# A two-block transformer on one core: another order of work inside both mixers

## Chip, cores and metric

One core of a Trainium2 chip runs the whole kernel. The metric is the device time of one execution in microseconds (us); the time before is a median of three runs. The engines are TensorE (PE, its weight loads PEld), VectorE (DVE), ScalarE (ACT), GpSimd (POOL) and SyncE (SP, which issues most transfers).

## The reference

Batch 1, 256 tokens, width 1024, two layers of a first block and two of a second, all in fp32. What matters here are the two mixers:

```python
# first block, layer l: x = x + 0.5*ffn; x = x + mixer; x = x + 0.5*ffn; x = rmsnorm(x)
# mixer: one projection gives q, k, v (3 groups of 8 heads), the input of a gated convolution, and gates
for g, (window, dil) in enumerate(DILATION_GROUPS):
    o, l = dilated_window_attn(q[:, :, g], k[:, :, g], v[:, :, g], dil, window // (2 * dil))
y_conv = conv_module(glu_in, conv_w, conv_b, conv_ln_g, conv_ln_b, ...)   # 31 taps, layer norm, silu
return (g_attn * y_attn + g_conv * y_conv) @ w_out
# second block, layer l
p = rmsnorm_2(x, norm1[l]) @ w_in[l]          # columns: u (512), q (512), k (128), v (128)
y_f = fft2(u).real @ w_f + b_f                # Fourier half
y_a = windowed_gqa(rope(rmsnorm_2(q)), rope(rmsnorm_2(k)), v, sink[l])
x = x + concat([rmsnorm_2(y_f), rmsnorm_2(y_a)]) @ w_o[l]   # then a gated ffn
```

## The kernel before

Weights stream from HBM in units of 128x1024 fp32 (512 KB, issued on SP by `fetch`). Each unit is split in two fp32r halves: ACT writes the high half (`wh`, L317) and DVE the low half (`wl`, L318); PE then makes three products (low x high, high x high, high x low) of each operand. `token_major` (L576) is the form with tokens on the partitions: 512 output columns, four units of 12 matmuls, with two PSUM banks, one for each half t of the tokens.

**Order of the program.** The functions are written out in the order in which they should run; a scheduler places each instruction in its engine's queue, and each engine works through its queue in that order. So a step whose input is late blocks what is queued behind it on the same engine. PSUM has a ring of `acc` and one of `aux` banks; a matmul into a bank waits until the bank's last reader is done.

**Block one, `mixer` (L630).** After the gated convolution's input, nine projections run in the order of `QKV` (L47): each pair is (0 q, 1 k, 2 v; group). For q and k, `head_norm_rope` normalises each head and rotates it: squares on ACT, the factor `rs` by a power on POOL (L548), four DVE operations of 128x512 (L554, L556, L558, L560). Each half is then transposed on PE (`transpose_to`, L572), queued in `turn` until the next projection is through. v needs only one DVE operation for each half (L767). The convolution is a product with tables of cosines: `conv_forward` after projection 2, `conv_inverse(0)` after 4, `conv_inverse(1)` within 5 (L715 and L719 are its matmuls, L725 its last DVE operation). Its layer norm starts in the attention: `norm_mean` adds up eight blocks, takes the mean by one PE product with ones (L375), subtracts it (L734) and squares (L367, L368). The attention has steps of scores (L796), softmax on DVE and ACT (L803 to L811), transposes (L913, copied out by ACT in L915) and products with v (L821), with gate units between.

**Block two, `mixer2` (L923).** The stream gives q (four units), then k and v together (two units), then the Fourier half u (four units). `rc` and `vc`, the inverse norm and the mean square of each token, are taken before. q and k go through `head_norm_rope`, u is split into `uh` and `ul` (L346, L347). Then come, between the attention's steps (table `fill`): `f1`, the transform over the channels, `f2`, the one over the tokens (tables 2 x 512 KB in the stream, split like weights; its input `Ah`, `Al` split too, three fp32r products each, L1010 to L1030), the product with `w_f`, and the output projection. Before layer 0, `rf` and eight multiplications (L1279) make the residual. `sink`, eight numbers of the layer, comes by a POOL transfer into `nsink` (L929) and is copied on DVE (L931).

Of the kernel before, what the change touches and what calls it, by code (L numbers as in the profile page):

```python
# [23 lines left out]
F32 = mybir.dt.float32  # L24
# [4 lines left out]
P = 128  # L29
# [58 lines left out]
def weight_stream(a):  # L88
# [113 lines left out]
class Kernel:  # L202
# [64 lines left out]
    def make_units(self):  # L267
# [12 lines left out]
        for l in range(DEPTH):  # L280
# [3 lines left out]
            add("w", 16 + 4 * 3, 1024)  # L284
            add("d", 1, FWD)
            add("w", 4 * 6 + 16 + 4 + 8 + 8, 1024)
            add("w", 44, 1024)
            add_down()
        for l in range(DEPTH):
# [3 lines left out]
            add("d", 2, 1024)  # L293
# [282 lines left out]
    def token_major(self, o, evac, mid=()):  # L576
# [4 lines left out]
        for q in range(4):  # L581
# [9 lines left out]
            if q == 1:  # L591
                for f in mid:
                    f()
# [36 lines left out]
    def mixer(self, l, x, o, sacc, prep):  # L630
# [96 lines left out]
        def norm_mean():  # L727
# [26 lines left out]
        after = {2: conv_forward, 4: lambda: conv_inverse(0)}  # L754
        mid = {5: [lambda: conv_inverse(1)]}

        turn = []
        qT, kT, vv = [None] * 3, [None] * 3, [None] * 3
        for j, (which, g) in enumerate(QKV):
# [86 lines left out]
        for i in range(len(steps) + 2):  # L846
# [4 lines left out]
            gate(*gates.pop(0))  # L851
            if soft1 is not None:
# [70 lines left out]
    def mixer2(self, l, x, o, rc, vc, prep):  # L923
# [17 lines left out]
        nc.vector.tensor_scalar_mul(evc, vc, EPS)  # L941

        turn = []
# [7 lines left out]
        self.token_major(o, evac_q)  # L951
# [13 lines left out]
        todo, turn = turn, []  # L965
        for t in range(2):
            z = self.t2("z")
            nc.scalar.activation(z[:, :128], acc[t][:, :128], AF.Copy)
            nc.scalar.activation(vt[:, t * P:(t + 1) * P], acc[t][:, 128:256], AF.Copy, scale=rc[:, t:t + 1])
# [7 lines left out]
        Ah, Al = self.t4("Ah", F32R), self.t4("Al", F32R)  # L977
# [5 lines left out]
        def f1(hf):  # L983
# [14 lines left out]
            self.split(a.rearrange("p (b c) -> p b c", b=2), Ah[:, fb], Al[:, fb])  # L998


        def f2(i):


            wh, wl = self.unit(1024)
            a = self.acc()
            p, q, e = a[:, :130], a[:, 130:258], a[:4, 258:388]
            for fb in range(4):
                for cs, (out, ts) in enumerate(((p, slice(0, 130)), (q, slice(128, 256)))):
                    c = slice((fb * 2 + cs) * P, (fb * 2 + cs + 1) * P)
                    self.mm3(out, wh[:, c], wl[:, c], Ah[:, fb, ts], Al[:, fb, ts], fb == 0 and cs == 0, fb == 3, skip=True)  # L1010
# [3 lines left out]
            nc.scalar.activation(q_, q[:, 1:], AF.Copy)  # L1014
# [6 lines left out]
            if i == 0:  # L1021

                alt = dftu[0][0][:, 512:516]
                for fb in range(4):
                    for A in (Ah, Al):
                        mm(e, alt, A[:, fb, :130], start=False, stop=fb == 3 and A is Al, skip_group_check=True)
# [291 lines left out]
```

## Time and profile before

| | |
|---|---|
| median of 3 runs | 1970.82 us (1970.71 to 1971.87) |
| the profiled execution | 1971.52 us, span of the trace 1969.7 us |
| instructions | 36890 |
| busy: DVE, ACT, POOL | 1417.5 us (72%), 1100.1 us (56%), 110.9 us (6%) |
| read from HBM | 334.99 MB, 171 GB/s over the span |
| mean granted clock of TensorE | 0.992 of full |

How to read it: PE is the engine that is nearly always at work, so the time is its work plus its gaps, plus what it loses where its clock is granted at half. A gap is read from the wait rows, which name the engine, its line, and the instruction that released it.

### The profile page before, as it was taken

To read this page: it belongs to the slowest core of one execution; us is meant where nothing else is said; L and a number is where in the kernel's file an instruction comes from. 1 tells how busy PE (TensorE), PEld (TensorE's weight loads), DVE (VectorE), ACT (ScalarE), POOL (GpSimd) and SP (SyncE) were. 2 spreads that over 40 slices of the span, in tenths; PEclk is the share of its full clock that TensorE was granted. 3 is DMA by queue.
4 is the path that set the end of the run, shared out by engine and by line. 5 is a ranking of instruction groups with operands and counts; after the bars stand their busy time and mean duration, and the time that the engine had idled before them with its cause. 6 is when DMAs were issued, how large, how long until landed. Compare 5 with 4: busy or idle time off the path is not lost.

```text
span 1969.7 us, 36890 instructions
## 1 busy us (share of the span) xinstructions
PE 1929.9 (98%) x14640; PEld 1832.0 (93%) x14640; DVE 1417.5 (72%) x2470; ACT 1100.1 (56%) x2125; POOL 110.9 (6%) x109
## 2 busy tenths in 40 slices
PE   8999999999999999999999999999899999999999
PEld 8999878899999999998787999999789999889999
DVE  6765787877666586656877676665779985779973
ACT  5544555666544455445556665444676764666652
POOL 1000022100000010000222000000200000100000
PEclk9999999999999999999999999999989999999999
DMA  8555654435555555556544345555424555434554
GB/s 266 192 179 184 212 190 150 156 129 173 181 182 177 187 177 185 175 185 218 172 166 138 119 172 184 182 175 190 147 85 166 190 183 180 156 108 168 196 176 125
DMA packets 97260, 338.43 MB, mean 172 GB/s; under 512 B 11430, under 2 KB 14086, under 8 KB 96960
## 3 DMA queue, kind: packets, MB, share of 16 engines
q1 hardware_dynamic: 93024, 325.97, 48.7%
q0 software_dynamic: 2944, 8.11, 1.8%
q8 instruction: 114, 1.87, 0.4%
q10 hardware_dynamic: 1120, 2.00, 0.3%
q14 instruction: 58, 0.48, 0.1%
HBM read 334.99 MB, written 1.05 MB: 171 GB/s over the span
## 4 chain that ended last, share of the span: by engine, by line
PE 78%; DVE 8%; issue 6%; POOL 3%; ACT 3%; DMA 1%; POOLq 0%; DVEq 0%; ACTq 0%
PE acc L335 23%; PE acc L337 23%; PE acc L336 23%; POOL rs L548 3%; DVE wl L318 2%; PE acc L588 2%; PE acc L590 2%; PE acc L589 2%; ACT wh L317 1%; PE pt L913 1%; PE Y L821 1%; PE s L796 1%; DVE ra L554 1%; DVE rb L556 1%; ACT sq L367 1%
## 5 line engine op out<-in xcount | busy, mean ns | idle before, releaser
L318 DVE TENSOR_TENSOR wl<-raw,wh 128x1024 fp32r<-128x1024 f32 (+2 forms) x632 | 756.6, 1199 | 326.1 <-ACT wh L317 321.8
L317 ACT ACTIVATE wh<-raw 128x1024 fp32r<-128x1024 f32 (+2 forms) x632 | 653.2, 1037 | 595.2 <-PE acc L337 268.4
L335 PE MATMUL acc<-xh,wl 128*128 128x256 f32 x1760 | 503.8, 286 | 5.6 <-DVE wl L318 5.6
L336 PE MATMUL acc<-xh,wh 128*128 128x256 f32 x1760 | 499.8, 284 | 0.0
L337 PE MATMUL acc<-xl,wh 128*128 128x256 f32 x1760 | 499.3, 284 | 0.0
L335 PEld LDWEIGHTS acc<-xh,wl 128*128 128x128 f32 x1760 | 339.3, 193 | 9.3 <-DVE wl L318 6.0
L336 PEld LDWEIGHTS acc<-xh,wh 128*128 128x128 f32 x1760 | 339.4, 193 | 0.3
L337 PEld LDWEIGHTS acc<-xl,wh 128*128 128x128 f32 x1760 | 339.2, 193 | 0.0
L335 PE MATMUL acc<-hh,wl 128*128 128x256 f32 x1056 | 298.8, 283 | 0.0
L336 PE MATMUL acc<-hh,wh 128*128 128x256 f32 x1056 | 298.8, 283 | 0.0
L337 PE MATMUL acc<-hl,wh 128*128 128x256 f32 x1056 | 298.8, 283 | 0.0
L335 PEld LDWEIGHTS acc<-hh,wl 128*128 128x128 f32 x1056 | 202.8, 192 | 0.0
L336 PEld LDWEIGHTS acc<-hh,wh 128*128 128x128 f32 x1056 | 202.8, 192 | 0.0
L337 PEld LDWEIGHTS acc<-hl,wh 128*128 128x128 f32 x1056 | 202.8, 192 | 0.0
L588 PE MATMUL acc<-wl,xh 128*128 128x512 f32 x480 | 189.1, 394 | 0.8 <-DVE wl L318 0.5
L590 PE MATMUL acc<-wh,xl 128*128 128x512 f32 x480 | 187.3, 390 | 0.0
L589 PE MATMUL acc<-wh,xh 128*128 128x512 f32 x480 | 187.0, 390 | 0.0
L337 PE MATMUL acc<-xn,wh 128*128 128x256 f32 x608 | 172.7, 284 | 1.2 <-DVE xn L344 1.2
L335 PE MATMUL acc<-xn,wl 128*128 128x256 f32 x608 | 172.5, 284 | 0.0
L336 PE MATMUL acc<-xn,wh 128*128 128x256 f32 x608 | 172.0, 283 | 0.0
L337 PEld LDWEIGHTS acc<-xn,wh 128*128 128x128 f32 x608 | 116.6, 192 | 2.1 <-DVE xn L344 2.0
L335 PEld LDWEIGHTS acc<-xn,wl 128*128 128x128 f32 x608 | 116.7, 192 | 0.6 <-ACT xn L343 0.5
(276 smaller groups left out, 2926.6 us busy)
## 6 DMA issues: line engine op xcount, KB each, us to landing
raw<-wts SPq DMA_DIRECT2D x576, 512.0 KB, 3.3
raw<-wts SPq DMA_DIRECT2D x48, 384.0 KB, 3.0
brow<-b_in POOLq DMA_DIRECT2D x26, 256.0 KB, 3.9
raw<-dft SPq DMA_DIRECT2D x4, 512.0 KB, 3.5
tab<-tab ACTq DMA_DIRECT2D x1, 1024.0 KB, 7.5
out<-xn SPq DMA_DIRECT2D x8, 128.0 KB, 3.5
wraw<-conv_w POOLq DMA_DIRECT2D x6, 124.0 KB, 4.7
raw<-dft SPq DMA_DIRECT2D x2, 258.0 KB, 2.6
```

The costliest lines, as they stand in the source:

```text
L317: nc.scalar.activation(h[:, :n], r[:, :n], AF.Copy)
L318: nc.vector.tensor_tensor(lo[:, :n], r[:, :n], h[:, :n].bitcast(F32), op=ALU.subtract)
L335: mm(out, wl, xh, start=start, stop=False, **k)
L336: mm(out, wh, xh, start=False, stop=False, **k)
L337: mm(out, wh, xl, start=False, stop=stop, **k)
L367: nc.scalar.activation(q, x, AF.Square, **kw)
L548: nc.gpsimd.tensor_tensor(rs[:, :nh], vv[:, :nh], self.mhalf[:, :nh], op=ALU.pow)
L554: nc.vector.tensor_tensor(A3, z3, cg[:, None, :].to_broadcast([P, nh, HD]), op=ALU.mult)
L556: nc.vector.tensor_tensor(half(B[:, :nh * HD]), half(zz)[:, :, ::-1, :], sg.rearrange("p (c d) -> p c d", c=2)[:, None].to_broadcast([P, n ...
L588: mm(accs[t], xh[k][:, ts], wl[:, c], start=k == 0, stop=False)
L589: mm(accs[t], xh[k][:, ts], wh[:, c], start=False, stop=False)
L590: mm(accs[t], xl[k][:, ts], wh[:, c], start=False, stop=k == KB - 1)
```

## The change

Block one: the order of `QKV` puts each v between q and k; a projection's second transpose is held until two units of the next projection are through; the convolution's steps start one projection earlier (`conv_forward` after 1, the inverses after 3 and 4), its sum of blocks (`conv_sum`) and mean (`conv_mean`) follow at 4 and 6, so that only the subtraction is left in the attention. The last held transposes run after the first gate.

Block two: the weight stream and the program have the order q, Fourier half, k and v. The norm's sums (`stats`) are taken behind q's fourth unit, the residual behind the second unit of the Fourier half. `f1` and the transposes of q and k run before the attention's first step. The tables of `f2` are read as fp32 by two transfers of their own and are not split; `f1`'s result is one fp32 tile `A`; `f2` multiplies in fp32, once for each piece.

```diff
-QKV = [(0, 0), (1, 0), (2, 0), (2, 1), (0, 1), (1, 1), (0, 2), (1, 2), (2, 2)]
+QKV = [(0, 0), (2, 0), (1, 0), (0, 1), (2, 1), (1, 1), (0, 2), (1, 2), (2, 2)]
...
-        parts += [_wide(w[:, 512:1024]), w[:, 1024:].reshape(2, 4, P, 256).transpose(0, 2, 1, 3), _wide(w[:, :512])]
+        parts += [_wide(w[:, 512:1024]), _wide(w[:, :512]), w[:, 1024:].reshape(2, 4, P, 256).transpose(0, 2, 1, 3)]
...
-            add("d", 2, 1024)
...
-            if q == 1:
-                for f in mid:
-                    f()
+            for f in mid.get(q, ()):
+                f()
...
-        def norm_mean():
+        def conv_sum():
             cs = self.rp.tile([P, S], F32, tag="sacc", name=self.nm("cs"))
...
-            M = self.mean_rows(cs, D, 0.0)
+            stat["cs"] = cs
+
+        def conv_mean():
+            stat["cm"] = self.mean_rows(stat["cs"], D, 0.0)
+
+        def norm_mean():
             for b in range(KB):
-                nc.vector.tensor_tensor(cb(b), cb(b), M, op=ALU.subtract)
+                nc.vector.tensor_tensor(cb(b), cb(b), stat["cm"], op=ALU.subtract)
...
-        after = {2: conv_forward, 4: lambda: conv_inverse(0)}
-        mid = {5: [lambda: conv_inverse(1)]}
+        after = {1: conv_forward, 3: lambda: conv_inverse(0), 4: lambda: (conv_inverse(1), conv_sum()), 6: conv_mean}
...
-            self.token_major(o, evac, mid.get(j, ()))
-            for f in todo:
+            self.token_major(o, evac, {1: held})
+            held = todo[1:]
+            for f in todo[:1]:
                 f()
...
+            if i == 0:
+                for f in held:
+                    f()
...
-    def mixer2(self, l, x, o, rc, vc, prep):
+    def mixer2(self, l, o, stats, residual, prep):
...
+                t = self.t4("fw").rearrange("p a b -> p (a b)")
+                o_ = P * (FWD + INV + 516) + i * P * UMAX
+                nc.sync.dma_start(t, self.a["dft"][o_:o_ + P * UMAX].rearrange("(p n) -> p n", p=P))
...
-        self.token_major(o, evac_q)
+        self.token_major(o, evac_q, {2: [tables], 3: [start]})
+        self.token_major(o, lambda t, a: self.split(a, uh[t], ul[t], st["rc"][:, t:t + 1]), {1: [lambda: x.extend(residual())]})
...
-        self.token_major(o, lambda t, a: self.split(a, uh[t], ul[t], rc[:, t:t + 1]), todo)
-        for f in turn:
-            f()
...
-            self.split(a.rearrange("p (b c) -> p b c", b=2), Ah[:, fb], Al[:, fb])
+            nc.scalar.activation(A[:, fb], a.rearrange("p (b c) -> p b c", b=2), AF.Copy)
...
-                    self.mm3(out, wh[:, c], wl[:, c], Ah[:, fb, ts], Al[:, fb, ts], fb == 0 and cs == 0, fb == 3, skip=True)
+                    mm(out, w[:, c], A[:, fb, ts], start=fb == 0 and cs == 0, stop=fb == 3, skip_group_check=True)
...
-        fill = {0: [lambda: f1(0)], 1: [lambda: f1(1), lambda: f2(0)], 2: [lambda: f2(1), lambda: (f3(0), f3(1))],
-                3: [lambda: (f3(2), f3(3)), later("s", lambda: self.square_sum([yf[:, b] for b in range(4)]))],
+        fill = {0: [lambda: f2(0)], 1: [lambda: f2(1)], 2: [lambda: (f3(0), f3(1)), lambda: (f3(2), f3(3))],
+                3: [lambda: proj(0, 0), lambda: proj(0, 1), later("s", lambda: self.square_sum([yf[:, b] for b in range(4)]))],
...
+        f1(0)
+        for f in turn[:2]:
+            f()
+        f1(1)
+        for f in turn[2:]:
+            f()
...
+            return self.rsqrt_small(vc, 2), vc
+
+        def residual():
+            rf = self.rows(self.rsqrt_small(keep["v1"], 2))
```

Three places of the queues show it. In a row stand the line, the operation, what is written and what is read, and the shape. First DVE in block one's second layer, from the last rotation of k (L560) to the first softmax (L803, L809 after the change); `sink` is the copy of block two's eight numbers, L738 the subtraction of the mean, L368 the sum of squares. Before:

```order
L318 TENSOR_TENSOR wl_11917<-raw_11860,wh_11916 128x1024
L560 TENSOR_TENSOR z_11823<-ra_11839,rs_11837 128x512
L931 TENSOR_SCALAR sink_16013<-nsink_16011 128x8
L932 TENSOR_SCALAR nsink_16011<-nsink_16011 128x8
L318 TENSOR_TENSOR wl_11980<-raw_11878,wh_11979 128x1024
L318 TENSOR_TENSOR wl_12010<-raw_11896,wh_12009 128x1024
L767 SCALAR_TENSOR_TENSOR qkv_11857<-acc_11858,rc_10529,brow_11724 128x512
L767 SCALAR_TENSOR_TENSOR qkv_11857<-acc_11859,rc_10529,brow_11724 128x512
L318 TENSOR_TENSOR wl_12063<-raw_11914,wh_12062 128x1024
L803 ISA e_11964,m_11966<-s_11956,tab 128x512
```

Now, from the first softmax on:

```order
L318 TENSOR_TENSOR wl_12075<-raw_11926,wh_12074 128x1024
L809 ISA e_11970,m_11972<-s_11962,tab 128x512
L809 ISA m_11972 128x1
L809 ISA e_11971,m_11972<-s_11963,tab 128x512
L809 ISA m_11972 128x1
L738 TENSOR_TENSOR conv_11322<-conv_11322,var_11728 128x256
L811 TENSOR_SCALAR m_11972<-m_11972 128x2
L738 TENSOR_TENSOR conv_11322<-conv_11322,var_11728 128x256 x2
L368 TENSOR_TENSOR sacc_12124<-sacc_12124,sq_12126 128x256
L940 TENSOR_SCALAR sink_15980<-nsink_15978 128x8
L368 TENSOR_TENSOR sacc_12124<-sacc_12124,sq_12129 128x256
```

The copy of `sink` moved from ahead of four splits and the first softmax to behind it; subtractions and sums of squares moved in between the first softmax and the second.

Second, PE in block two's first layer where k is transposed (`tr` from `zk`, one for each half), with `f1` (L994 to L996 before, L1011 to L1013 now) and the scores (`s`). Before:

```order
L590 MATMUL acc_16242<-wh_16263,xl_15929 128x512
L572 MATMUL tr_16331<-ident,zk_16206 128x128 x2
L572 MATMUL tr_16335<-ident,zk_16225 128x128 x2
L994 MATMUL acc_16388<-wh_16293,uh_16016 128x256
L994 MATMUL acc_16434<-wh_16293,uh_16016 128x256
L995 MATMUL acc_16388<-wh_16293,ul_16017 128x256
```

Now:

```order
L1011 MATMUL acc_16366<-wh_16227,uh_15983 128x256
L1012 MATMUL acc_16366<-wh_16227,ul_15984 128x256
L1013 MATMUL acc_16366<-wl_16228,uh_15983 128x256
L572 MATMUL tr_16380<-ident,zk_16288 128x128 x2
L1026 MATMUL acc_16419<-A_16323,fw_16045 128x129
L572 MATMUL tr_16384<-ident,zk_16307 128x128 x2
L1026 MATMUL acc_16419<-A_16323,fw_16045 128x127
L1026 MATMUL acc_16419<-A_16323,fw_16045 128x129
L1026 MATMUL acc_16419<-A_16323,fw_16045 128x127
L1107 MATMUL s_16388<-kT_15986,qT_15985 128x256
```

`f1` stood behind the transposes of k and right behind u; it stands ahead of them now, with q's eight transposes, and the four units of u lie ahead of k and v.

Third, DVE at the same place: `zk` is k after its rotation, `sink` the copy for the layer after, `e` the first softmax. Before:

```order
L565 TENSOR_TENSOR zk_16225<-ra_16234,rs_16232 128x2x64 x2
L318 TENSOR_TENSOR wl_16385<-raw_16261,wh_16384 128x1024
L931 TENSOR_SCALAR sink_19616<-nsink_19614 128x8
L932 TENSOR_SCALAR nsink_19614<-nsink_19614 128x8
L318 TENSOR_TENSOR wl_16466<-raw_16291,wh_16465 128x1024
L347 SCALAR_TENSOR_TENSOR ul_16017<-acc_16241,rc_16009,uh_16016 128x512
L347 SCALAR_TENSOR_TENSOR ul_16017<-acc_16242,rc_16009,uh_16016 128x512
```

Now:

```order
L565 TENSOR_TENSOR zk_16288<-ra_16297,rs_16295 128x2x64 x2
L318 TENSOR_TENSOR wl_16596<-raw_16255,wh_16595 128x1024
L546 TENSOR_SCALAR vv_16312<-ss_16308,evc_15988 128x2
L554 TENSOR_TENSOR ra_16316<-z_16304,ropec_14000 128x128
L556 TENSOR_TENSOR rb_16317<-z_16304,ropes_14001 128x128
L558 TENSOR_TENSOR ra_16316<-ra_16316,rb_16317 128x128
L565 TENSOR_TENSOR zk_16307<-ra_16316,rs_16314 128x2x64 x2
L940 TENSOR_SCALAR sink_19562<-nsink_19560 128x8
L941 TENSOR_SCALAR nsink_19560<-nsink_19560 128x8
L1113 ISA e_16394,mx_16396<-s_16388,tab 128x256
```

The copy of `sink` stood ahead of `ul` and stands ahead of the first softmax now.

## Rows read from the trace of the kernel before

**Rows 1.** the page: busy us and share of engines; granted clock, 40 slices

```profile
PE 1929.9 (98%) x14640; PEld 1832.0 (93%) x14640; DVE 1417.5 (72%) x2470; ACT 1100.1 (56%) x2125; POOL 110.9 (6%) x109
...
PEclk9999999999999999999999999999989999999999
```

**Rows 2.** windows: stretch, length, busy of each engine, clock, DMA share, GB/s

```profile
345.00:393.00 48.00, 45.42 (x288) 39.37 (x287) 40.66 (x76) 32.57 (x105) 9.18 (x5) 1.00 0.48 160
1031.00:1079.00 48.00, 43.69 (x251) 36.63 (x250) 38.13 (x69) 30.36 (x101) 10.06 (x6) 0.93 0.48 159
1387.00:1425.00 38.00, 32.11 (x172) 26.44 (x171) 30.37 (x69) 26.22 (x79) 10.78 (x7) 0.99 0.41 134
1425.00:1450.00 25.00, 23.50 (x135) 19.34 (x136) 18.36 (x71) 16.06 (x49) 0.00 (x0) 0.74 0.24 85
1706.00:1738.00 32.00, 26.76 (x178) 21.43 (x177) 24.06 (x81) 20.78 (x58) 0.87 (x1) 0.95 0.39 132
```

**Rows 3.** timeline of PE, block one, layer 0: two waits, in brackets

```profile
371.58 0.63 PE L572 MATMUL tr<-ident,z 128*128 128x128 f32 x4 [1.12 <-DVE z L560]
...
386.75 0.71 PE L796 MATMUL s<-qkv,qkv 64*128 64x256 f32 x6 [1.46 <-ACT pT L915]
```

**Rows 4.** PE's waits in 1031 to 1079 (block one, layer 1)

```profile
PE sum L375 <- DVE m L803: 2.5, 1, 2.5
PE tr L572 <- DVE z L560: 1.1, 1, 1.1
PE s L796 <- ACT pT L915: 0.7, 1, 0.7
```

**Rows 5.** groups of instructions: count, busy us, mean ns, idle before

```profile
L368 DVE TENSOR_TENSOR sacc<-sacc,sq 128x256 f32<-128x256 f32 x110 | 45.0, 420 | 2.5
...
L715 PE MATMUL acc<-inv,Y 128*128 128x128 f32 x64 | 8.3, 277 | 2.9 <-DVE conv L725 2.9
```

**Rows 6.** timeline of PE, inverse convolution: start, length

```profile
315.54 1.95 PE L715 MATMUL acc<-inv,Y 128*128 128x128 f32 x16
```

**Rows 7.** timeline of PE, end of f1 and start of f2, layer 1

```profile
1716.64 0.28 PE L995 MATMUL acc<-wh,ul 128*128 128x256 f32 x1
1716.76 0.28 PE L996 MATMUL acc<-wl,uh 128*128 128x256 f32 x1
...
1717.16 0.27 PE L335 MATMUL acc<-Ah,wl 128*128 128x128 f32 x1
...
1717.72 0.27 PE L337 MATMUL acc<-Al,wh 128*128 128x130 f32 x1
```

**Rows 8.** timeline of POOL, block two, layer 0

```profile
1418.12 0.59 POOL L929 DMA_DIRECT2D nsink<-sink  x1
```

**Rows 9.** timeline of DVE, the same place

```profile
1418.61 1.22 DVE L318 TENSOR_TENSOR wl<-raw,wh 128x1024 fp32r<-128x1024 f32 x1
1422.66 0.17 DVE L931 TENSOR_SCALAR sink<-nsink 128x8 f32<-128x8 f32 x1 [2.83 <-DMA nsink<-sink]
...
1424.09 1.40 DVE L347 SCALAR_TENSOR_TENSOR ul<-acc,rc,uh 128x512 fp32r<-128x512 f32 x2
```

**Rows 10.** PE's waits in 1420 to 1450 (block two, layer 0)

```profile
PE acc L995 <- DVE ul L347: 2.7, 1, 2.7
PE acc L994 <- ACT uh L346: 2.1, 1, 2.1
```

**Rows 11.** PE's waits in 1706 to 1738 (block two, layer 1)

```profile
PE acc L335 <- ACT yfh L343: 1.7, 1, 1.7
PE pt L913 <- DVE e L1114: 1.1, 1, 1.1
```

**Rows 12.** timeline of ACT: k's second half leaves PSUM, layer 1

```profile
1702.26 0.26 ACT L968 ACTIVATE z<-acc 128x128 f32<-128x128 f32 x1
```

**Rows 13.** timeline of DVE: k's second half is done, layer 1

```profile
1708.17 0.49 DVE L565 TENSOR_TENSOR zk<-ra,rs 128x128 f32<-128x128 f32 x2 [0.27 <-POOL rs L548]
```

**Rows 14.** line 1279, the residual: count, shortest, median, longest in ns

```profile
L1279 DVE SCALAR_TENSOR_TENSOR xn<-xn,vec,R x8: 474/476/477, 1397.9 to 1400.6; 128x256 f32<-128x256 f32 x8
```

More of the change, by code (lines that the diff above doesn't have):

```diff
@@ L283, in make_units @@
             pos["d"] = 0
-            add("w", 16 + 4 * 3, 1024)
+            add("w", 16 + 4 * 2, 1024)
             add("d", 1, FWD)
-            add("w", 4 * 6 + 16 + 4 + 8 + 8, 1024)
+            add("w", 4 * 7 + 16 + 4 + 8 + 8, 1024)
             add("w", 44, 1024)
@@ L940, in mixer2, with start, tables @@
         evc = self.small("evc", 2)
-        nc.vector.tensor_scalar_mul(evc, vc, EPS)
-        turn = []
+        st, turn, x, fw = {}, [], [], []
+        def start():
+            st["rc"], vc = stats()
+            nc.vector.tensor_scalar_mul(evc, vc, EPS)
+        def tables():
+            for i in range(2):
+                t = self.t4("fw").rearrange("p a b -> p (a b)")
+                o_ = P * (FWD + INV + 516) + i * P * UMAX
+                nc.sync.dma_start(t, self.a["dft"][o_:o_ + P * UMAX].rearrange("(p n) -> p n", p=P))
+                fw.append(t)
         def evac_q(t, a):
@@ L964, in mixer2 @@
                     mm(acc[t][:, :256], xl[k][:, ts], wh[:, c], start=False, stop=k == KB - 1)
-        todo, turn = turn, []
         for t in range(2):
@@ L997, in f1 @@
             fb = slice(hf * 2, hf * 2 + 2)
-            self.split(a.rearrange("p (b c) -> p b c", b=2), Ah[:, fb], Al[:, fb])
+            nc.scalar.activation(A[:, fb], a.rearrange("p (b c) -> p b c", b=2), AF.Copy)
         def f2(i):
-            wh, wl = self.unit(1024)
+            w = fw[i]
             a = self.acc()
-            p, q, e = a[:, :130], a[:, 130:258], a[:4, 258:388]
+            p, q, e = a[:, :129], a[:, 129:256], a[:4, 256:385]
             for fb in range(4):
-                for cs, (out, ts) in enumerate(((p, slice(0, 130)), (q, slice(128, 256)))):
+                for cs, (out, ts) in enumerate(((p, slice(0, 129)), (q, slice(129, 256)))):
                     c = slice((fb * 2 + cs) * P, (fb * 2 + cs + 1) * P)
-                    self.mm3(out, wh[:, c], wl[:, c], Ah[:, fb, ts], Al[:, fb, ts], fb == 0 and cs == 0, fb == 3, skip=True)
+                    mm(out, w[:, c], A[:, fb, ts], start=fb == 0 and cs == 0, stop=fb == 3, skip_group_check=True)
+            if i == 0:
+                alt = dftu[0][0][:, 512:516].bitcast(F32)
+                for fb in range(4):
+                    mm(e, alt, A[:, fb, :129], start=False, stop=fb == 3, skip_group_check=True)
             y = self.t2("yF")
@@ L1013, in f2 @@
             q_ = y[:, 257:384]
-            nc.scalar.activation(q_, q[:, 1:], AF.Copy)
+            nc.scalar.activation(q_, q, AF.Copy)
             tt(y[:, 1:128], p[:, 1:128], q_, op=ALU.add)
@@ L1021, in f2 @@
             if i == 0:
[L1023 to L1026, printed above, removed]
                 self.split(e[:1, :129], yh[:1, 2, :129], yl[:1, 2, :129])
@@ L1160, in mixer2 @@
             proj(1, ob)
+        return x
     def ffn2(self, l, x, meanwhile=None):
@@ L1275, in run, with stats @@
         sa, sb = self.square_sum(x), self.square_sum(x, gf[1])
-        v1 = self.mean_cols(sa, D, EPS)
-        rf = self.rows(self.rsqrt_small(v1, 2))
-        for b in range(KB):
-            nc.vector.scalar_tensor_tensor(x[b], x[b], gf[1][b], rf, op0=ALU.mult, op1=ALU.mult)
-        vg = self.mean_cols(sb, D, 0.0)
-        vc = self.combine_v(v1, vg)
+        keep = {}
+        def stats():
+            keep["v1"] = self.mean_cols(sa, D, EPS)
+            vc = self.combine_v(keep["v1"], self.mean_cols(sb, D, 0.0))
+            return self.rsqrt_small(vc, 2), vc
+        def residual():
+            rf = self.rows(self.rsqrt_small(keep["v1"], 2))
+            for b in range(KB):
+                nc.vector.scalar_tensor_tensor(x[b], x[b], gf[1][b], rf, op0=ALU.mult, op1=ALU.mult)
+            return x
         for l in range(DEPTH):
-            rc = self.rsqrt_small(vc, 2)
-            self.mixer2(l, x, o, rc, vc, prep2[l])
+            x = self.mixer2(l, o, stats, residual, prep2[l])
             self.ffn2(l, x, None if l else lambda: prep2.append(self.mixer2_prep(1)))
@@ L1287, in run, with stats @@
                 o = self.operand(x, self.gains(1, "norm1_2"))
-                vc = self.mean_cols(self.square_sum(x), D, EPS)
+                s1 = self.square_sum(x)
+                def stats():
+                    vc = self.mean_cols(s1, D, EPS)
+                    return self.rsqrt_small(vc, 2), vc
+                residual = lambda: x
         assert self.used == len(self.units)
```

12 lines of the change are left out of this document (6 added, 6 removed).

## The prediction

> **What bounds the kernel.** I read the page first, then the windows of the stretches that the change touches, then PE's waits in each, and the timelines last. The page [rows 1] says that PE is busy 1929.9 of 1969.7 us: all its gaps come to 39.8 us, and no other engine is above 72%. So the change can gain only by PE's gaps in the two mixers, by PE work that goes away, and by what TensorE loses where its clock is granted below full speed. The windows [rows 2] show where that is. In block one the same stretch, 48 us long, has 288 matmuls at a clock of 1.00 in layer 0 and 251 at 0.93 in layer 1: 37 fewer, at 0.12 us each (the distance of two matmuls of 256 columns, [rows 7]) some 4.4 us that layer 1 loses against layer 0. In block two's layer 0 the 25 us from 1425 have a clock of 0.74: part of them at 2.4 GHz and part at 1.2 GHz, which costs 25 x 0.26 = 6.5 us, and in the 38 us before them PE is idle 5.9. In layer 1 the 32 us from 1706 have 5.2 us of idle time and 0.95, which is 1.6 us.
>
> The waits name the causes. Block one: a transpose on the end of k's rotation (1.1 us in both layers), the inverse convolution on the operation before it (2.9 us for two, [rows 5], so 1.4 in each layer), a score on a free PSUM bank (1.5 in layer 0, 0.7 in layer 1), and in layer 1 alone 2.5 us in which the mean of the convolution (L375) stands in PE's queue before its input is there [rows 3, 4]. Block two, layer 0: `f1` waits 2.1 us for `uh` and 2.7 us for `ul` [rows 10]. The second has a cause off PE: DVE stands 2.83 us on `sink`, whose POOL transfer was issued at 1418.12 and landed at 1422.66, 4.5 us later, and `ul` is queued behind it [rows 8, 9]. Layer 1: the largest waits are 1.7 us on `yfh` and 1.1 us on a softmax [rows 11].
>
> **The change, part by part.**
>
> *Block one, layer 0.* Gone: 1.4 (the convolution has a projection of v, without rotation, beside it), 1.1 (the last transposes of k lie behind v's four units) and 1.5 (the old bank wait), together 4.0 us. New: v0 stands directly before the forward convolution, whose first products need the banks that v0 leaves, and the second half of v1 needs a bank behind a rotation. The trace has no such wait; between nothing and the 2.5 us that PE waited for DVE in the same stage [rows 4] I take 1.5, since DVE is the more loaded with v there. Also new: the sum of squares stands between the first softmax and the second. Seven additions of 0.42 us [rows 5] are 2.9 us on DVE; from nothing to 2.9 reach PE beside the old 1.5. I take 3.0 for both. 4.0 - 4.5 = -0.5 us, between -4 and +2.
>
> *Block one, layer 1.* The same, and the 2.5 us of L375 go too, because the mean is taken two projections earlier; with 0.7 for the bank wait, 1.4 + 1.1 + 2.5 + 0.7 = 5.7 us of waits, and 48 x 0.07 = 3.4 us of clock, 9.1 in all. Against them the same 4.5, and I leave 1.1 of the clock's loss standing: +3.5 us, between 0 and 5.7 + 3.4 - 1.5 = +7.6.
>
> The copy of `sink` in layer 1 moves behind the first softmax, where its transfer has had longer. The work that it let wait is then the additions, which nobody on PE needs soon.
>
> *Block two, layer 0.* Gone are the 2.1 and 2.7 us: u ends two units of k and v before `f1`. What is late next is k. Its second half takes from 1702.26, when it leaves PSUM, to 1708.66, the end of its rotation [rows 12, 13], 6.4 us in layer 1. Ahead of its transpose PE now has 24 matmuls of `f1` at 0.12 and eight transposes at about as much, 3.8 us. So PE waits 6.4 - 3.8 = 2.6 us, and if the two halves run one after the other on DVE (a split of 1.22 [rows 9], four small operations and the power between them) up to 3.4 more. I take 5 of these 6.0. The eight multiplications of the residual, 8 x 0.476 = 3.8 us [rows 14], stood ahead of q's rotation and now stand between u's units and k and v's, where a split of a weight is queued behind them; 1.5 us, between 0 and 3.8. The DVE queue stops at `sink` again, now ahead of the first softmax: the transfer still comes after the last power of k, some 4.5 us. PE has `f2`, 16 fp32 products, and two scores to do then, about 5.5 us, which covers it. Idle time before: 5.9 + 1.5 = 7.4; after: 6.5, and 0.9 is gained. The work of `f2`: before, 56 fp32r matmuls of at most 130 columns at 0.112 us (five steps from 1717.16 to 1717.72, [rows 7]) = 6.3; now 20 in fp32. The inverse convolution is such a product: 64 instructions for 32 products, 16 in 1.95 us [rows 5, 6], 0.24 each: 20 x 0.24 = 4.8. So 1.5 us less in each layer. The clock: 6.5 us lost before; the new gaps are of the same size and it falls again, but for a shorter stretch, as the work behind them is dense: 1.1 gained, between -2 and +6.5. Sum 0.9 + 1.5 + 1.1 = +3.5 us, between -3 and +9.
>
> *Block two, layer 1.* No residual and no `sink` here. Gone: 1.7 and 1.1 us and some smaller waits, 5.2 in all; new: k's 2.6 + half of 3.4 = 4.3. With the 1.5 of `f2` and a clock loss of 2.0 in place of 1.6, 5.2 - 4.3 + 1.5 - 0.4 = +2 us; if the clock falls as in layer 0 (6.5), -2.5, and at best +6.
>
> *At nothing.* Two splits fewer in each layer, since the tables go straight to SBUF, save ACT and DVE work beside PE's; the tables move the same bytes earlier, and these stretches draw 85 to 160 GB/s [rows 2]. `rc` behind q's fourth unit is covered by u's units.
>
> **Sum.** -0.5 + 3.5 + 3.5 + 2 = 8.5 us. The profiled execution took 1971.52, so 1963.0; the median of the runs shown lies 0.7 below it, and by the median I forecast 1962.3 us, 0.43% less. A measurement of this kernel can tell about 0.2%, 3.9 us, from no change.
>
> **fp32 in `f2`.** The rows above price an fp32 product of 128 columns at 0.24 us, 2.1 times one fp32r matmul. The Trainium skill, page "FP8 and Floating Point Precision", section "TensorE Precision Notes", says that true fp32 takes four passes through the array. Read as four times the fp32r matmul beside it, that would be 0.45 us a product, and 9.0 us for a layer's 20: 2.7 more than before in place of 1.5 less. It is the first rival below; by the rows I take 0.24.
>
> **Rivals.**
> - *fp32 at four times fp32r.* 4 x 0.112 x 20 = 9.0 us against 6.3: 4.2 us a layer worse than in my sum, 8.4 for both: 1970.7. Against it stand the 64 instructions of the inverse convolution, measured in this kernel.
> - *k eats block two's gain.* The two waits for k come to the full 6.0 us in both layers, with the clock down as before: block two's 5.5 us are lost, 1967.8. For it speaks that k is now the last projection before the scores, and that POOL's power and the splits stand in its chain. The Trainium skill, page "SBUF — State Buffer", says that a DVE operation with two inputs from SBUF and a GpSimd operation that reads it shut each other out of a shared port; a split beside k's power would by that add up to its 1.2 us to each half. The split of 1.22 us beside a power is no longer than the others here, so the trace leaves that open.
> - *The clock stays full in block two's layer 0.* Then 5.4 us more come back, 1956.9. For it: u's four units and q stand without a gap before k.
> - *Slower.* In block one, the scores of the attention's second and third step wait on the second softmax, which stands behind four subtractions and seven additions on DVE. If the two waits come within a few us and reach 2.5 us together with the forward convolution's, as in layer 1 of before, the clock falls in both layers: layer 0 comes to -0.5 - 3.4 = -3.9, layer 1 gains nothing, and block two nothing as in the rival above: 1970.8 + 3.9 = 1974.7. The point from which it decides is whether the transposes of the first probabilities (L913) are reached with DVE more than 2.5 us behind. Against it: layer 0 took a wait of 1.5 at the same place with a clock of 1.00.
>
> **Chances.** Forecast 0.48 (its own range 1958 to 1966.9), full clock 0.15, k eats it 0.18 (two fifths of it just under the bound of 1966.9), fp32 0.04, no net change for other reasons 0.04, slower 0.11. So faster 0.48 + 0.15 + 0.07 = 0.70, same 0.11 + 0.04 + 0.04 = 0.19, slower 0.11. The range from 1954.5 to 1971.5 leaves out the slower case and the best tenth of the best one.
>
> **What would show it.** Right: no wait of L375 after the first softmax in block one's layer 1, and a clock near 1.00 in its attention; in block two no wait on `uh` or `ul` but waits of k's transposes on `zk`, 2 to 6 us together; `f2` of 16 instructions in some 1.9 us. Wrong: waits of v's units or scores in block one of over 4.5 us a layer, `f2`'s instructions at 0.2 us or more, or a wait of DVE on `sink` that reaches PE.

## The result and the profile after

The changed kernel takes 1949.69 us (median of 4 runs, 1948.61 to 1950.04) against 1971.18 us before (4 runs): a ratio of 0.989, 95% interval 0.9873 to 0.9907. It is 21.5 us faster; the forecast was 8.5 us, and its range began at 1954.5. The profiled execution has a span of 1948.2 us, 21.5 less than before. A measurement here tells apart some 0.15 to 0.2%, and the starts of two executions of one program text differ (the first token-major matmul stands at 205.5 us after the change and 206.2 before, though nothing ahead of it was edited). So the stages below are taken from the profiles, each from landmark to landmark: a mixer of block one from its first 512-column matmul to the first sum onto the residual (DVE, L908 before), one of block two from its first 512-column matmul to the first sum of the ffn behind it (L1208 before). What lies between the stages is equal to 0.1 us.

| stage | before | after | difference | forecast |
|---|---|---|---|---|
| block one, layer 0 | 279.6 | 278.0 | -1.6 | +0.5 |
| block one, layer 1 | 284.1 | 279.0 | -5.1 | -3.5 |
| block two, layer 0 | 238.8 | 231.4 | -7.4 | -3.5 |
| block two, layer 1 | 230.3 | 223.6 | -6.7 | -2 |

With the 0.7 us of the start that makes 21.5. All four stages gained more than forecast. The page after, its busy line and the granted clock in 40 slices:

```profile
PE 1915.2 (98%) x14608; PEld 1823.4 (94%) x14608; DVE 1407.4 (72%) x2462; ACT 1095.4 (56%) x2121; POOL 112.6 (6%) x109
...
PEclk9999999999999999999999999999999999999999
```

PE is busy 14.7 us less [rows 1]: its gaps, 33.0 us now, gave 6.8, and the rest is work that left or ran at a higher clock. The windows that answer to [rows 2], moved by as much as the stage before them gained (layer 1 of block one by 2, block two by 7 and 16):

```profile
345.00:393.00 48.00, 46.12 (x296) 40.74 (x297) 42.39 (x83) 33.32 (x109) 9.62 (x5) 0.96 0.49 160
1029.00:1077.00 48.00, 46.11 (x304) 40.65 (x304) 43.08 (x86) 32.80 (x108) 10.18 (x6) 1.00 0.50 166
1380.00:1418.00 38.00, 33.74 (x192) 29.18 (x191) 31.79 (x67) 26.60 (x80) 7.46 (x7) 0.99 0.44 153
1418.00:1443.00 25.00, 23.94 (x164) 20.02 (x164) 16.40 (x81) 18.16 (x59) 0.00 (x0) 0.88 0.09 33
1690.00:1722.00 32.00, 30.08 (x235) 26.51 (x235) 23.75 (x94) 24.28 (x79) 1.57 (x2) 1.00 0.29 99
```

The columns are those of [rows 2]. In block one layer 1 now has 304 matmuls where it had 251, at a clock of 1.00; layer 0 has a little more than before and a clock of 0.96. In block two layer 0 the clock of the second stretch rose from 0.74 to 0.88, and layer 1 lost 3.3 us of idle time and runs at 1.00. PE's waits over the whole span that lie in the mixers (engine, line, who released it: us in total, times, longest):

```profile
PE s L802 <- ACT qkv L573: 3.8, 2, 1.9
PE tr L572 <- DVE zk L565: 2.9, 3, 1.0
PE acc L588 <- DVE z L773: 2.2, 2, 1.1
PE acc L335 <- ACT yF L1039: 2.1, 2, 1.1
...
PE acc L1026 <- ACT A L1015: 1.8, 1, 1.8
...
PE acc L691 <- DVE qkv L770: 1.6, 2, 1.4
```

Of the waits of [rows 3, 4, 10] only 0.4 us on a score's bank are left. In their place stand a score that waits 1.9 us in each layer of block one for k's copy out of PSUM, v's second bank (1.1 us in each), the forward convolution on the bank that v0 leaves (L691, 0.2 us in layer 0 and 1.4 in layer 1), k's transposes in block two (2.9 us in three waits), and `f2` on its input A (1.8). The product behind `f2` [rows 11] still waits 1.1 us in each layer for ACT (`yF`). What stands on ACT ahead of k's copy in layer 0 of block one (PE's score comes at 371.38):

```profile
369.48 0.42 ACT L367 ACTIVATE sq<-conv 128x256 f32<-128x256 f32 x1 [1.20 <-DVE conv L738]
369.81 1.04 ACT L317 ACTIVATE wh<-raw 128x1024 fp32r<-128x1024 f32 x1
370.75 0.58 ACT L573 ACTIVATE qkv<-tr 128x512 f32<-128x512 f32 x1
```

A square that waits for DVE's subtraction and a split of a weight are queued ahead of the copy. PE's step of `f2`:

```profile
1425.86 2.05 PE L1026 MATMUL acc<-A,fw 128*128 128x129 f32 x16
```

These 16 instructions are 8 fp32 products, two instructions each: 2.05 us are 0.26 us for a product, against 0.24 in the prediction.

### The profile page after: what moved, and what is told of

Same layout as the page of the kernel before. It is cut to its first block, busy times and chain, and to the rows that moved or that the text cites. A ratio compares the mean times of both kernels' runs of the same rounds, so it can differ in the third digit from the quotient of the medians.

```text
span 1948.2 us, 36799 instructions
## 1 busy us (share of the span) xinstructions
PE 1915.2 (98%) x14608; PEld 1823.4 (94%) x14608; DVE 1407.4 (72%) x2462; ACT 1095.4 (56%) x2121; POOL 112.6 (6%) x109
## 4 chain that ended last, share of the span: by engine, by line
PE 79%; issue 8%; DVE 6%; POOL 3%; ACT 2%; DMA 2%; POOLq 0%; SPq 0%; DVEq 0%; ACTq 0%
PE acc L335 23%; PE acc L337 23%; PE acc L336 23%; POOL rs L548 2%; PE acc L588 2%; PE acc L589 2%; PE acc L590 2%; DVE wl L318 1%; PE pt L922 1%; ACT wh L317 1%; PE s L802 1%; PE Y L827 1%; DMA x<-x 1%; ACT sq L367 1%; DMA raw<-wts 1%
```

## The experiments

Differences of the stages against the kernel before, in us, each from one profile:

| kernel | one, 0 | one, 1 | two, 0 | two, 1 | median of runs |
|---|---|---|---|---|---|
| the changed kernel | -1.6 | -5.1 | -7.4 | -6.7 | 1949.69 |
| b1_only | -1.6 | -6.1 | +1.4 | 0.0 | 1962.42 |
| b2_only | 0.0 | +0.1 | -8.5 | -6.8 | 1957.22 |
| f2_only | 0.0 | -0.1 | -4.8 | -5.9 | 1960.85 |
| f2_split | -1.8 | -6.2 | -3.4 | -0.9 | 1958.39 |
| f2_tabs | -1.7 | -6.0 | -4.9 | -4.0 | 1954.02 |
| v_behind | +5.3 | +2.3 | -8.1 | -6.4 | 1962.44 |
| no_hold | -0.4 | -4.8 | -7.5 | -5.0 | 1951.71 |
| mean_early | +1.1 | -4.4 | +1.9 | -0.7 | 1967.06 |
| sink_early | +0.1 | -4.4 | -3.8 | -0.8 | 1964.44 |
| res_late | -1.8 | -6.0 | -10.4 | -6.9 | 1946.21 |
| both_late | -3.0 | -4.9 | -9.0 | -4.9 | 1947.72 |
| res_sink | -1.5 | -6.2 | -11.6 | -5.0 | 1949.56 |
| res_sink_sq | -2.0 | -6.5 | -11.9 | -5.2 | 1949.03 |
| res_sq | -2.1 | -5.3 | -9.8 | -6.4 | 1946.51 |

Stages whose code is that of the kernel before or of a sister differ by up to 2 us (b1_only and mean_early in block two's layer 0; both_late against res_late in its layer 1), and where they do the clock differs. A stage's difference under 2 us is therefore not told apart by one profile. The kernel before, run beside these experiments, has medians of 1971.73 to 1972.48 us against the 1971.18 above, so a median of this table may stand 0.5 to 1.3 us too high beside 1949.69.

**The two blocks alone** (b1_only, b2_only): the parts of the diff for one block, on the kernel before.

```diff
 # b1_only: QKV, token_major, mixer and the stream's places for them
-QKV = [(0, 0), (1, 0), (2, 0), ...
+QKV = [(0, 0), (2, 0), (1, 0), ...
...
 # b2_only: mixer2, its stream, stats and residual
```

> Only block one's part of the change, on the kernel before (block two, its stream and f2 as before). Theory A, read from the trace of the changed kernel: the two mixers of block one give about 7 of the 21.5 us (the last sums of layer 0 come 2.4 us earlier, those of layer 1 another 5.1, of which 0.7 were already there before the first mixer): 1964, with the mean's product (L375) no longer waiting in layer 1 and the clock at 1.00 there. Rival, the prediction's terms: -0.5 and +3.5 us, 1968.

> Only block two's part, on the kernel before. Theory A: 7.4 us in layer 0 and 6.7 in layer 1, 1957. Rival, the prediction's terms 3.5 and 2: 1965.7. If b1_only and b2_only together give less than 21.5 us by over 2 us, the two parts help each other.

b1_only 1962.42 us (ratio 0.9952, 0.9939 to 0.9966), b2_only 1957.22 (0.9924, 0.9912 to 0.9936). Theory A on both: 7.7 us in block one's stages, 15.3 in block two's, together 2.2 more than in the changed kernel. By the medians they come to 10.1 and 15.3, 3.8 more than its 21.5, which the intervals still cover. So neither part needs the other, and the prediction was too low in each.

**f2's form** (f2_split, f2_tabs, f2_only): the first undoes it in the changed kernel; the second keeps fp32 on PE, but has the tables in the stream and split again, and leaves their low half out of the products; the third makes it alone in the kernel before.

```diff
 # f2_split, against the changed kernel
+            add("d", 2, 1024)
...
-            nc.scalar.activation(A[:, fb], a.rearrange("p (b c) -> p b c", b=2), AF.Copy)
+            self.split(a.rearrange("p (b c) -> p b c", b=2), Ah[:, fb], Al[:, fb])
...
-                    mm(out, w[:, c], A[:, fb, ts], ...)
+                    self.mm3(out, wh[:, c], wl[:, c], Ah[:, fb, ts], Al[:, fb, ts], ...)
 # f2_tabs, against the changed kernel
+            add("d", 2, 1024)
...
-            w = fw[i]
+            w = self.unit(1024)[0].bitcast(F32)
```

> The changed kernel with f2 as before: its tables in the stream and split, Ah and Al, three fp32r products a piece. Theory A: only PE's work in f2 differs, 2 x 1.2 to 1.5 us, so about 1952.5. Rival: the two splits a layer and the tables' places in the stream matter too (ACT and DVE stand in k's chain just there): 1955 or more.

> The changed kernel with the tables of f2 in the stream and split as before, but f2 in fp32 on one tile A, with the high half of the tables alone (the low half is made and left out of the products). So PE does f2 as the changed kernel does it, while ACT and DVE do the splits of before. Theory D: what f2_split lost beyond PE's 2.7 us is the splits' time on ACT, where the evacuation of f2 and the halves yfh wait (3.4 us of f3's wait in layer 1): about f2_split less 2.7, 1955 to 1956. Rival E: it is PE, the 56 narrow fp32r products, whose stretch runs at the lower clock: about the changed kernel, 1950 to 1951.

> The kernel before with f2's part alone: fp32 on one tile A, tables by two transfers of their own and not split; the order of block two as before. Theory F: the fp32 form and the missing splits help wherever f2 stands between the scores, 4 to 5 us a layer: 1962 to 1964. Rival G: in the old order f1 waits for uh, ul and sink anyway, and only PE's 1.5 us a layer go: 1968 to 1969, so that the rest is due to the new order.

f2_split 1958.39 us (0.9931, 0.9919 to 0.9944), f2_tabs 1954.02 (0.9907, 0.9894 to 0.9921), f2_only 1960.85 (0.9946, 0.9934 to 0.9958). So f2's form is worth 8.7 us by the medians in the changed kernel (7.4 when each is taken against the kernel before beside it), of which about half comes with PE's form (4.4) and half with the tables' splits and their place in the stream (4.3), two things that no run takes apart; alone in the old order it is worth 10.7 us by the stages. Theories D and E each hold half; F holds, G falls. PE's waits of f2_split, f2_tabs and f2_only in the stretch of block two's layer 1 that answers to [rows 11], in this order:

```profile
PE acc L336 <- ACT yfh L344: 3.4, 1, 3.4
PE acc L1036 <- DVE e L1124: 1.5, 1, 1.5
```

```profile
PE pt L923 <- DVE e L1123: 1.6, 1, 1.6
```

```profile
PE pt L912 <- DVE e L1120: 0.7, 1, 0.7
PE acc L1002 <- DVE ul L346: 0.7, 1, 0.7
```

In f2_split the product behind f2 waits 3.4 us for `yfh` (1.7 before), which ACT makes, and in f2_split and f2_tabs a product or a softmax's transpose waits 1.5 to 1.6 for `e`; in f2_only the waits on `yfh` are gone and two of 0.7 remain. ACT's rows of f2_split ahead of that wait, with the second f2's copies out of PSUM (`yF`):

```profile
1715.17 0.21 ACT L1113 ACTIVATE se<-se 128x4 f32<-128x4 f32 x1 [0.60 <-DVE se L1112]
...
1715.78 0.26 ACT L1024 ACTIVATE yF<-acc 128x127 f32<-128x127 f32 x1
1715.93 1.04 ACT L318 ACTIVATE wh<-raw 128x1024 fp32r<-128x1024 f32 x1
...
1718.09 0.72 ACT L344 ACTIVATE yfh<-yF 128x256 fp32r<-128x256 f32 x2
```

A split of 1.04 us stands between the first copy and `yfh`, and ACT had waited 0.6 us for a number of the softmax that DVE made behind a split. In the kernel before a split of that length lies at the same place; in the changed kernel none does, and the product waits 1.1 us. (Between the first f2's copies all three have one, so that one explains nothing.) In f2_tabs the place is another one, ACT ahead of the first exponentials of layer 1:

```profile
1704.78 1.06 ACT L318 ACTIVATE wh<-raw 128x1024 fp32r<-128x1024 f32 x1 [2.44 <-PE acc L1019]
1705.85 1.28 ACT L1112 ACT_TABLE_LOAD   x1
...
1707.26 0.49 ACT L1116 ACTIVATE e<-e,nm 128x256 f32<-128x256 f32 x1
```

Here a split waits 2.44 us for f2's own product (L1019), and ACT's load of its table for the exponentials, 1.28 us, is queued behind it. In the changed kernel that load was over 1.6 us before the first exponential had its input. So PE waits 1.6 us for `e` in both layers of f2_tabs: not the split's time alone, but the buffer that it waits for and the load behind it. The clock goes along: windows of f2_only in layer 0 and 1 of block two, then of f2_split in layer 0.

```profile
1424.00:1449.00 25.00, 23.71 (x150) 17.93 (x151) 17.81 (x81) 14.49 (x49) 0.00 (x0) 0.87 0.18 64
1701.00:1733.00 32.00, 30.60 (x209) 23.81 (x208) 24.43 (x96) 22.96 (x71) 0.87 (x1) 1.00 0.31 100
```

```profile
1413.00:1437.00 24.00, 21.76 (x100) 18.15 (x101) 17.58 (x67) 16.31 (x49) 1.42 (x2) 0.57 0.31 107
```

f2_only has 0.87 and 1.00 where [rows 2] have 0.74 and 0.95; f2_split runs 24 us at 0.57, most of them at 1.2 GHz, though PE idles only 2.2 us in them. Each is one profile, and the section on what was not expected shows how far the clock scatters.

**The order of block one** (v_behind, no_hold): the changed kernel with the old `QKV`, and with no transposes held.

```diff
 # v_behind
-QKV = [(0, 0), (2, 0), (1, 0), (0, 1), (2, 1), (1, 1), (0, 2), (1, 2), (2, 2)]
+QKV = [(0, 0), (1, 0), (2, 0), (2, 1), (0, 1), (1, 1), (0, 2), (1, 2), (2, 2)]
 # no_hold
-            held = todo[1:]
-            for f in todo[:1]:
+            held = []
+            for f in todo:
```

> The changed kernel with the old QKV order (v behind k), transposes still held and the convolution's steps at their new numbers. Theory: v's units cover the rotations; without them the last k's transposes and the convolution wait for rotations again, 1 to 2 us a layer: 1952 to 1954. Rival: the held transposes and the early mean do it alone: 1949 to 1950.

> The changed kernel with no transposes held: both halves right behind the next projection. Theory: with v between q and k only k's second half is late, 3 times in a layer at most 0.7 to 1.1 us: 1951 to 1954, and the first scores no longer wait for a copy of the held half. Rival: holding costs as much in restarts as it saves, 1949 to 1950.

v_behind 1962.44 us (0.9943, 0.993 to 0.9957): some 12 us worse than the changed kernel, several times what was expected, and its block one is slower than before the change. PE's waits in its layer 1, and the granted clock of a stretch in layer 0 and of one in layer 1:

```profile
PE s L802 <- ACT qkv L573: 3.5, 1, 3.5
PE tr L572 <- DVE z L560: 2.2, 2, 1.8
```

```profile
372.00:384.00 12.00, 8.59 (x53) 7.83 (x52) 11.93 (x25) 7.09 (x15) 1.75 (x1) 0.72 0.68 219
968.00:980.00 12.00, 9.11 (x25) 6.21 (x25) 10.96 (x18) 2.59 (x12) 4.22 (x5) 0.57 0.21 69
```

Transposes among the forward convolution's products wait for rotations again, 2.2 us in two waits. The first scores wait 3.5 us for k's copy on ACT, 1.6 more than in the changed kernel; the rotation of this k was over before PE came to its transpose, so this wait is not the rotation's, and why ACT comes to the copy later stays open. The two stretches at 0.72 and 0.57 lose 3.4 and 5.2 us more. With the old order the earlier convolution does not pay: v's place between q and k is needed. no_hold 1951.71 (0.9893, 0.9879 to 0.9907) cannot be told from the changed kernel: waits on `z` come back (1.4 us in three, in each layer), and in place of the one on k's copy a score waits 1.4 us for DVE's softmax. Whether holding pays stays open.

**Layer 1 of block one** (mean_early, sink_early): on the kernel before, the mean taken early alone, and `sink` loaded before the first mixer alone.

```diff
 # mean_early
-        after = {2: conv_forward, 4: lambda: conv_inverse(0)}
+        after = {2: conv_forward, 4: lambda: conv_inverse(0), 5: conv_sum, 7: conv_mean}
 # sink_early
-        nc.gpsimd.dma_start(nsink, ...)
+        sink, nsink = self.sinks[l]
```

> The kernel before, with the sum of the convolution's blocks after projection 5 and its mean (L375) after projection 7 in place of the attention's second step; all else as before. Theory: in layer 1 the 2.5 us of L375, 0.7 of a score and 2.7 us at half clock go, in layer 0 nothing: 1971.5 - 5 = 1966. Rival: the subtractions come earlier too and stand ahead of the first softmax, and a score waits as it does in the changed kernel (1.9 us in each layer): 1970 to 1972.

> The kernel before, with both layers' sink loaded and copied before the first mixer, into tiles of their own. Theory of the prediction: in layer 0 of block two ul no longer stands behind 2.8 us of DVE's wait; PE's 2.7 us on ul go and some of the clock's 6.2 us: 1966 to 1968. Rival: uh's wait of 2.1 us and the clock's drop stay, only part of ul's wait goes: 1970.

mean_early 1967.06 us (0.9978, 0.9969 to 0.9987), sink_early 1964.44 (0.9964, 0.9952 to 0.9977). In block one's layer 1 either takes 4.4 us, so each is enough there. PE's waits at the place of [rows 4], of mean_early and then of sink_early:

```profile
PE s L801 <- DVE m L808: 0.8, 1, 0.8
PE s L801 <- ACT qkv L573: 0.6, 1, 0.6
```

```profile
PE s L797 <- ACT pT L916: 1.4, 1, 1.4
PE tr L573 <- DVE z L561: 1.1, 1, 1.1
```

The 2.5 us of L375 had DVE's softmax as their releaser, and that softmax stood behind `sink` (and behind three splits, not four), where DVE had waited in the kernel before:

```profile
1059.62 0.17 DVE L931 TENSOR_SCALAR sink<-nsink 128x8 f32<-128x8 f32 x1 [2.49 <-DMA nsink<-sink]
```

With `sink` out of the way L375 waits no longer, though it is where it was, and the waits are those of layer 0 [rows 3]. In block two's layer 0 sink_early took another 3.8 us, where 3 to 5 were expected in the whole kernel.

**The residual and k's chain** (res_late): the residual's multiplications behind the third step of the fill.

```diff
-        self.token_major(o, lambda t, a: ..., {1: [lambda: x.extend(residual())]})
+        self.token_major(o, lambda t, a: ...)
-        fill = {..., 2: [lambda: (f3(0), f3(1)), lambda: (f3(2), f3(3))],
+        fill = {..., 2: [lambda: (f3(0), f3(1)), lambda: (f3(2), f3(3)), lambda: x.extend(residual())],
```

> The changed kernel with the residual's sums and eight multiplications (layer 0 of block two) behind the third step of the attention's fill instead of behind the second Fourier unit. Theory B: the multiplications hold back a split, the split holds back the weight buffers, SP stops issuing, and ACT stands 4.9 and 2.4 us on weights with k's copy out of PSUM queued behind: without them k's waits (1.0 and 1.0 us) and f2's wait on A (1.8) mostly go, and with them the clock's 3 us: 1944 to 1946. Rival C: k's chain is late by its own rotation and power: 1949 to 1950, the waits on zk as they are.

1946.21 us (0.9869, 0.9856 to 0.9883). In the changed kernel DVE multiplies eight times ahead of a split, SP's queue stands on splits, and ACT on weights that have not come; its rows, DVE's and ACT's, and SP's waits in 1395 to 1425:

```profile
1402.13 2.86 DVE L1309 SCALAR_TENSOR_TENSOR xn<-xn,vec,R 128x256 f32<-128x256 f32 x7
1404.90 1.22 DVE L318 TENSOR_TENSOR wl<-raw,wh 128x1024 fp32r<-128x1024 f32 x1
```

```profile
1409.46 1.06 ACT L317 ACTIVATE wh<-raw 128x1024 fp32r<-128x1024 f32 x1 [4.92 <-DMA raw<-wts]
1410.42 0.26 ACT L988 ACTIVATE z<-acc 128x128 f32<-128x128 f32 x1
...
1413.78 1.06 ACT L317 ACTIVATE wh<-raw 128x1024 fp32r<-128x1024 f32 x1 [2.37 <-DMA raw<-wts]
1414.74 0.26 ACT L988 ACTIVATE z<-acc 128x128 f32<-128x128 f32 x1
```

```profile
SPq L305 <- DVE wl L318: 27.5, 6, 17.0
```

The copies of k out of PSUM (L988) stand behind those 4.92 and 2.37 us. In res_late PE's waits in 1400 to 1432, and the window that answers to the fourth of [rows 2]:

```profile
PE tr L572 <- DVE zk L565: 1.3, 1, 1.3
PE acc L335 <- ACT yF L1039: 1.1, 1, 1.1
PE pt L922 <- DVE e L1130: 0.7, 1, 0.7
```

```profile
1418.00:1443.00 25.00, 23.28 (x176) 19.77 (x176) 20.64 (x82) 21.71 (x69) 0.00 (x0) 1.00 0.08 25
```

The wait on A is gone, k's waits went from 2.0 to 1.3, and the clock is at 1.00 (0.88): 3.0 us in the stage. Theory B holds for the wait on A and for the time; most of k's wait stays, as rival C had it.

**Scores on k's copy, sink, squares** (both_late, res_sink, res_sink_sq, res_sq), all on res_late.

```diff
 # both_late: the subtractions and the squares behind the first softmax
+            with self.tc.issue_after(stat["exp0"].ins), self.tc.issue_after(stat["dv0"].ins):
...
 # res_sink_sq, res_sq: the squares alone
+            with self.tc.issue_after(stat["exp0"].ins):
+                stat["cv"] = self.square_sum([cb(b) for b in range(KB)])
...
 # res_sink, res_sink_sq: as sink_early
+        sink, nsink = self.sinks[l]
```

> The kernel of res_late, and in block one the subtractions and squares of the norm behind the first softmax. Theory: the first scores wait 1.9 us in each layer for k2's copy out of PSUM, which stands on ACT behind squares that wait for DVE; with them later 3 to 4 us go, and the clock's drop there: profile 1940, median 1942. Rival: the softmax of the second step then waits in its turn for what is moved behind the first, and nothing is left, 1946.

> The kernel of res_late with sink loaded and copied before the first mixer. Theory: in the changed order DVE's wait on sink (2.4 us in layer 0 of block two) hides behind the scores, since the first softmax waits another 1.3 us for PE after it: nothing, 1946. Rival: it still reaches PE through the first softmax, 1943.

> The kernel of res_sink with the norm's squares alone (ACT) behind the first softmax's exponentials, the subtractions as in the changed kernel. Theory: the 1.9 us in which the first scores wait for k2's copy come from squares on ACT that wait for DVE ahead of that copy; both layers lose them, 3 to 4 us less than res_sink. Rival: the copy waits for the splits ahead of it too, half of it stays: 1 to 2 us less.

> res_late with the norm's squares behind the first softmax's exponentials, and sink loaded as in the changed kernel. In the stages of res_sink_sq block one took 0.3 and 0.5 us less than in res_late; its two transfers before the first mixer may have cost 2 to 3 us at the start. Theory: without them 1945 to 1946, just under res_late. Rival: the start scatters by itself, 1947 to 1949.

1947.72 (0.9876, 0.9861 to 0.9891), 1949.56 (0.988, 0.9867 to 0.9894), 1949.03 (0.9881, 0.9867 to 0.9894) and 1946.51 us (0.9867, 0.9852 to 0.9882): none is better than res_late beyond its scatter. For both_late the rival's time holds, though not by its softmax: the 1.9 us shrink to 0.4 in layer 0, and in layer 1 a score waits 2.3 us for the copy. In res_sq the scores of layer 0 wait 1.0 us for DVE's softmax and 0.7 for the copy. res_sink and res_sink_sq reach their first token-major matmul at 210.0 and 208.7 us, res_sq at 206.9; b2_only, with the start of the kernel before, has 208.2, so what the transfers of `sink` cost there is not settled. res_late and res_sq are the best versions here; res_late is the simpler.

## Why the prediction was wrong

**The bound and the place** were right: only PE's gaps, its work and its clock in the four mixer stages moved, and the waits named in [rows 3, 4, 10] went. The sign was right; the size, 8.5 us for 21.5, was not.

**The step that failed most** is the sentence "At nothing. Two splits fewer in each layer ... save ACT and DVE work beside PE's". f2_split has the new order with f2 as it was, and block two's stages gain 4.3 us by it, where the sum without f2's 3.0 has 2.5. With f2's new form they gain 14.1. So f2's form is worth 9.8 us there, 6.8 more than in the sum, out of 8.6 that the sum lacks in block two; alone, in f2_only, it is worth 10.7. f2_tabs prices what the sum had at nothing, the splits with the tables' place in the stream: 4.3 us by the medians, 2.5 and 2.7 by the stages. That work was not beside PE's: it stands in ACT's queue ahead of the exponentials and of `yfh`, and PE waits for both. [rows 11] showed those waits, 1.7 and 1.1 us, and the prediction listed them as gone without asking what made them.

**f2's work on PE** was right in itself: the steps of its matmuls, from each start to the next without the waits, come to 6.55 us in layer 1 before and 5.10 after, 1.45 less for 1.5 forecast. The rival on fp32 at four times fp32r falls by the row of f2 above: 0.26 us a product, 2.3 times the narrow fp32r matmul, not 4. The four passes of the Trainium skill, page "FP8 and Floating Point Precision", section "TensorE Precision Notes", are not four times the fp32r step of [rows 7]: a narrow fp32r matmul (0.112 us for 128 columns) takes almost as long as one of 256 (0.12).

**Block one, layer 0**, forecast +0.5, came to -1.6: the new waits were sized at 4.5 us, and are 1.1 (v1's bank) and 1.9 (a score), 3.0. And [rows 3] lie in a window that leaves out a second wait on a rotation, 0.7 us in each layer, that went too. PE's waits on `z` in the kernel before:

```profile
PE tr L572 <- DVE z L560: 3.6, 4, 1.1
```

The additions before the second softmax (2.9 of that term) were to lengthen the wait on a bank, which is 0.4 us in all; the wait that came is on k's copy, which ACT does behind a square and a split, and the prediction had not looked at ACT's queue there.

**Block one, layer 1**, -3.5, came to -5.1, by two causes of which each is enough. The new waits (1.9, 1.1 and 1.4 us) are the 4.5 of the sum; the clock, of which 1.1 us were left standing, came back whole (251 matmuls at 0.93 before, 304 at 1.00 now). The prediction gave the gain to the early mean. It said of `sink` that the copy moves behind the first softmax "where its transfer has had longer", and put no price on it; sink_early shows 4.4 us.

**Block two, layer 0**: the mechanism was right (u's waits go, k's come) and the waits close: PE's 5 for k came to 2.0 and 1.8 on A behind them, and the stage's idle time went from 8.5 to 7.8. The residual's 1.5 us on PE were 0.5 (its eight multiplications take 3.25 us on DVE and not 3.8, since each starts before the one ahead ends), but it acted through the weights' transfers on k instead, which the prediction did not see; res_late takes 3 us by it. The clock was sized at 1.1 us and gave 3.5 by the windows (25 us at 0.74, then at 0.88). With 0.7 of idle time and 1.4 of f2's work that makes 5.6 of the 7.4; the rest, in matmuls that are the same in both, stays open.

**Block two, layer 1**: k's wait, 4.3 us in the sum, was 0.9. The 6.4 us from PSUM to the end of the rotation were read [rows 12, 13] where DVE also rotated q; with q done long before, a chain that is k's alone is shorter, 3.5 us here (1695.84 to 1699.31). And the clock, for which 0.4 us of loss were put in, gained 1.6 (32 us at 0.95, then at 1.00).

**The rival that k eats the gain** left open whether a split beside k's power costs anything, since the split does not take longer there. The power does. POOL's power of k in block two's layer 0, in the kernel before with a split beside it, and in the changed kernel with none:

```profile
1416.15 2.00 POOL L548 TENSOR_TENSOR rs<-vv,mhalf 128x2 f32<-128x2 f32 x1 [2.21 <-DVE vv L546]
```

```profile
1412.72 0.70 POOL L548 TENSOR_TENSOR rs<-vv,mhalf 128x2 f32<-128x2 f32 x1 [11.23 <-DVE vv L546]
```

In the changed kernel no split fell beside either half's power (0.70 and 0.87 us), so this cost did not come.

**The slower rival** had its point at the first probabilities' transposes behind DVE. No such wait came in block one of any run shown here. v_behind shows a like outcome, scores that wait 3.5 us and the clock down in both layers, but by k's copy on ACT.

## What to carry to other kernels

Before a saving on an engine off the critical path is put at nothing, look at who waits for that engine in the same stretch: a 1 us operation that stands between a result in PSUM and its copy is on the path, and one that waits for a buffer holds up all that is queued behind it. A wait's releaser is the last link only; follow it one engine further (here from the mean's product to a softmax to a small transfer) before the gain is given to the edit that moves the waiter. Work moved to a quieter place on one engine can hold back the buffers of the weight stream, so check the transfers' waits behind it.

## What was not expected of the hardware

The same gap did not always bring the same clock. A score waits 1.9 us in both layers of block one, in the changed kernel and in res_late; the granted clock of the 8 us around it in layer 0 and in layer 1, of the changed kernel and then of res_late:

```profile
370.00:378.00 8.00, 6.62 (x43) 6.50 (x44) 7.93 (x18) 3.57 (x9) 0.00 (x0) 0.79 0.59 200
1054.00:1062.00 8.00, 6.11 (x54) 5.76 (x53) 8.00 (x17) 2.88 (x6) 0.14 (x1) 1.00 0.66 206
```

```profile
370.00:378.00 8.00, 6.76 (x56) 6.55 (x56) 7.93 (x19) 3.57 (x9) 0.00 (x0) 1.00 0.62 200
1054.00:1062.00 8.00, 6.75 (x44) 6.63 (x45) 8.00 (x21) 3.57 (x9) 0.00 (x0) 0.79 0.60 197
```

0.79 and 1.00 in the one, 1.00 and 0.79 in the other, with the same code there. So a gap of about 2 us costs between nothing and some 1.7 us more (8 us at 0.79), and the forecast of such a stretch has that width. And 24 us at a mean clock of 0.57 with PE idle for 2.2 of them (f2_split) show that the clock can stay low long after the gap: PE's waits ahead of them are 1.1, 1.6 and 0.6 us, and the changed kernel, with 1.0, 1.8 and 1.0 at the same place, has 25 us at 0.88. What brings it back was not tried.
